# Later conditioning of a hybrid decoder trunk: sums over the partitions by VectorE's block transposes, and one matmul for up to three parts

## The chip, the core and the metric

One NeuronCore of one Trainium2 chip runs the whole program. The metric is the device time of one execution in microseconds (us). In this text PE is TensorE's matrix part and PEld its weight loads, DVE is VectorE, ACT is ScalarE, POOL is GpSimd and SP is SyncE, whose queue issues most DMAs. L12 is line 12 of the kernel before, unless the text says that it is of the changed one.

## The reference

Four layers of a decoder trunk on x of 1024 positions by 1024 features, in float32. Layer i uses one mixer: layers 0 and 3 HGRN2 (a gated linear recurrence), layer 1 attention with a sliding window (SWA), layer 2 gated DeltaNet (GDN). A conditioning vector c sets a shift, a scale and a gate for each layer:

```
mod = (c @ ada_w[i] + ada_b[i])[:, None, :]        # 1024 x 3072 weights for each layer
shift, scale, gate = jnp.split(mod, 3, axis=-1)
h = rmsnorm(x, norm_g[i]) * (1.0 + scale) + shift
x = x + gate * mixer(h)
```

The change touches the first of these lines alone, for most of the layers: the vector times matrix product that gives the 3072 numbers of `mod`.

## The kernel before

The activations lie with features on the 128 partitions. The 3072 columns of `ada_w[i]` are worked in six parts of 512: parts 0 and 1 are the shift, 2 and 3 the scale, 4 and 5 the gate. Parts 0 to 3 of layer 0 are needed at once and go through `ada_first`, which neither version changes. The other twenty parts (4 and 5 of layer 0, all six of layers 1, 2 and 3) are the later conditioning. It is the generator `ada` (L407), which runs as a side stream beside the mixer of the layer before: `weave` takes a step of it now and then, 18 or 8 steps for each head of HGRN2, 16 for each group of SWA, 10 for each head of GDN, and what is left is drained at the mixer's end. Parts 4 and 5 of layer 0 and all of layer 1 run in layer 0, those of layer 2 in layer 1, those of layer 3 in layer 2.

A part has nine steps. In eight of them a tile of 128 rows by 512 columns of the matrix is loaded (L415) and DVE adds the tile, times c of that row, to the sum `acc` (L403, L405). Now acc holds, for each partition, a sum over eight rows; what is still to do is the sum over the 128 partitions, with the result turned so that columns come to lie on partitions. In the ninth step `ada_cols` (L421) does both by matmuls: four pieces of acc, 128 by 128 each, are the weights, a column of ones is the moving operand, and four columns of results come out in PSUM (L426). DVE adds the bias and writes them to `mod` (L428). After parts 2 and 3 DVE also makes `gcol`, the norm's weight times one plus scale (L432). `acc` has one buffer. The order of the parts is 2, 0, 3, 1, 4, 5.

Three resources are shared with the mixers:

- The matrix tiles are loaded into the tag "raw" of the pool wp, three buffers of 128x512. All weights come through the same three: `load_w` (L160) loads a raw tile, ACT rounds it to the part `w_hi` (L171), DVE makes the rest `w_lo` (L172), and three matmuls (L196 to L198) use the two parts. Those have four buffers each.
- The results of L426 go to a PSUM bank of the tag "tr", of which there is one. HGRN2's transposes `kh_ps` (L1077) and `ot_ps` (L1109), SWA's `qt_ps` (L1296) and GDN's transposes use it too.
- `eye32` (made at L272) is a constant of 128x128 that both versions have: four copies side by side and on top of each other of the identity of 32 by 32.

The order of instructions on each engine is set by a scheduler that places them by priority and by its own costs; each engine then works through its queue in that order. HGRN2's state matmul `s_ps` (L1092), SWA's query gate `sw_zs` (L1280) and HGRN2's `hg_zs` (L971) are the neighbours of which the prediction speaks.

## Time and profile before

| what | value |
|---|---|
| median of 3 runs | 2759.97 us (2746.81 to 2761.26) |
| the profiled execution | 2755.2 us |
| its span, first to last instruction | 2753.5 us |
| PE, DVE, ACT busy | 97%, 73%, 45% |
| the later conditioning's matmuls, first and last start | 135.9 and 1831.7 us |

The profile is that of one execution. A row of a group of instructions names the line, engine, operation, the tiles written and read and how many there are, then the busy time and the mean duration, and then the engine's idle time in front of them with what ended it. A row of the timeline gives the start, the duration, the engine and what it did, with an idle time ahead of it in brackets. A row of the waits names who waited for whom: the total, how many times, the longest. A row of windows gives the stretch, its length, and the busy time of PE, PEld, DVE, ACT and POOL, then PE's granted clock, the DMA share and GB/s.

### The profile page before, as it was taken

Reading aid. Unit: us, or ns where it says so; the run is one execution under the profiler, and the core shown is the slowest. Engines: PE = TensorE matmul, PEld = TensorE weight load, DVE = VectorE, ACT = ScalarE, POOL = GpSimd, SP = SyncE. Lnnn points to the kernel's source line nnn. Section 1 sums busy time; section 2 is a strip of 40 time slices with the busy share of each in tenths; the row PEclk is TensorE's granted clock in tenths of the full one; section 3 lists DMA queues with packets and bytes.
Section 4 is the critical chain, followed back from the end, with each engine's and each line's share of the span. In section 5 each row is a group of like instructions: output and inputs, shape, how many; then the busy total and the mean of one; then the engine's idle time right before and its main releaser. Section 6 shows DMA issues by size and latency. Waiting matters only on the chain.

```text
span 2753.5 us, 51775 instructions
## 1 busy us (share of the span) xinstructions
PE 2662.9 (97%) x19217; PEld 2147.3 (78%) x19217; DVE 1997.0 (73%) x5669; ACT 1235.4 (45%) x3139; POOL 136.5 (5%) x352
## 2 busy tenths in 40 slices
PE   8999999999999999899999999999999999999999
PEld 4878888778878767677787887787778888887877
DVE  6675765778677777777898898988775757556575
ACT  4332333344445565444445555555543434333342
POOL 0000100000000000001001001100000001000000
PEclk9999999999999999999999999999999999999999
DMA  6232222344223243334343343432454211111133
GB/s 240 77 104 79 70 79 76 109 133 150 58 89 100 74 147 93 111 82 107 97 127 85 104 126 93 124 101 80 142 183 127 85 51 43 51 43 51 46 119 112
DMA packets 347667, 273.30 MB, mean 99 GB/s; under 512 B 68964, under 2 KB 276247, under 8 KB 347415
## 3 DMA queue, kind: packets, MB, share of 16 engines
q1 hardware_dynamic: 347126, 268.95, 32.7%
q8 instruction: 151, 2.47, 0.4%
q14 instruction: 102, 0.83, 0.1%
q0 software_dynamic: 288, 1.05, 0.1%
HBM read 224.77 MB, written 45.15 MB: 98 GB/s over the span
## 4 chain that ended last, share of the span: by engine, by line
PE 74%; DVE 12%; DMA 6%; ACT 4%; issue 2%; SPq 0%; POOL 0%; DVEq 0%; ACTq 0%; POOLq 0%
PE proj_ps L196 10%; PE proj_ps L197 10%; PE proj_ps L198 10%; PE outp_ps L196 4%; PE outp_ps L198 4%; PE outp_ps L197 4%; PE projt_ps L196 3%; PE projt_ps L198 3%; PE projt_ps L197 3%; DMA ada_w<-in_ada_w_dram 2%; PE pv_ps L1340 1%; DVE gd_tb L617 1%; DVE w_lo L172 1%; DMA o_in<-od 1%; PE w_ps L859 1%
## 5 line engine op out<-in xcount | busy, mean ns | idle before, releaser
L196 PE MATMUL proj_ps<-hhi,w_hi 128*128 128x512 f32 x1664 | 682.2, 410 | 11.6 <-ACT gd_tb L615 8.4
L198 PE MATMUL proj_ps<-hhi,w_lo 128*128 128x512 f32 x1664 | 677.6, 408 | 1.3 <-issue 1.3
L197 PE MATMUL proj_ps<-hlo,w_hi 128*128 128x512 f32 x1664 | 676.8, 407 | 0.0
L196 PEld LDWEIGHTS proj_ps<-hhi,w_hi 128*128 128x128 f32 x1664 | 316.1, 190 | 69.4 <-ACT gd_tb L615 11.2
L198 PEld LDWEIGHTS proj_ps<-hhi,w_lo 128*128 128x128 f32 x1664 | 315.7, 190 | 57.7 <-issue 1.9
L197 PEld LDWEIGHTS proj_ps<-hlo,w_hi 128*128 128x128 f32 x1664 | 315.8, 190 | 56.3 <-issue 1.6
L172 DVE TENSOR_TENSOR w_lo<-w_raw,w_hi 128x512 fp32r<-128x512 f32 x332 | 223.2, 675 | 165.6 <-ACT w_hi L171 136.7
L171 ACT CAST w_hi<-w_raw 128x512 fp32r<-128x512 f32 x332 | 201.7, 611 | 293.6 <-PE proj_ps L197 167.9
L197 PE MATMUL projt_ps<-w_lo,hhi 128*128 128x256 f32 x896 | 257.4, 290 | 4.1 <-DVE w_lo L172 4.1
L196 PE MATMUL projt_ps<-w_hi,hhi 128*128 128x256 f32 x896 | 257.6, 290 | 0.8 <-ACT w_hi L171 0.8
L198 PE MATMUL projt_ps<-w_hi,hlo 128*128 128x256 f32 x896 | 256.1, 289 | 0.0
L196 PE MATMUL outp_ps<-o_hi,w_hi 128*128 128x512 f32 x576 | 229.1, 400 | 4.7 <-ACT o_hi L1166 3.6
L198 PE MATMUL outp_ps<-o_hi,w_lo 128*128 128x512 f32 x576 | 228.0, 398 | 1.6 <-DVE w_lo L175 1.6
L197 PE MATMUL outp_ps<-o_lo,w_hi 128*128 128x512 f32 x576 | 229.2, 399 | 0.2
L197 PEld LDWEIGHTS projt_ps<-w_lo,hhi 128*128 128x128 f32 x896 | 171.1, 192 | 7.1 <-DVE w_lo L172 5.2
L196 PEld LDWEIGHTS projt_ps<-w_hi,hhi 128*128 128x128 f32 x896 | 171.0, 192 | 4.2 <-ACT w_hi L171 1.2
L198 PEld LDWEIGHTS projt_ps<-w_hi,hlo 128*128 128x128 f32 x896 | 171.0, 192 | 2.7 <-issue 1.4
L617 DVE SCALAR_TENSOR_TENSOR gd_tb<-gd_xs,taps,gd_tb 128x512 f32<-128x512 f32 x192 | 144.3, 752 | 25.2 <-ACT gd_tb L615 21.3
L174 ACT ACTIVATE w_hi<-w_raw,par 128x512 fp32r<-128x512 f32 (+1 forms) x136 | 94.7, 698 | 140.1 <-PE outp_ps L197 95.5
L196 PEld LDWEIGHTS outp_ps<-o_hi,w_hi 128*128 128x128 f32 x576 | 108.6, 189 | 29.0 <-ACT o_hi L1166 5.7
L198 PEld LDWEIGHTS outp_ps<-o_hi,w_lo 128*128 128x128 f32 x576 | 109.0, 190 | 24.7 <-DVE w_lo L175 2.2
L175 DVE SCALAR_TENSOR_TENSOR w_lo<-w_raw,par,w_hi 128x512 fp32r<-128x512 f32 (+1 forms) x136 | 96.8, 716 | 41.6 <-ACT w_hi L174 39.9
(389 smaller groups left out, 4923.3 us busy)
## 6 DMA issues: line engine op xcount, KB each, us to landing
ada_w<-in_ada_w_dram SPq DMA_DIRECT2D x160, 256.0 KB, 2.8
w_raw<-in_hg_in_w_dram SPq DMA_DIRECT2D x136, 256.0 KB, 2.9
w_raw<-in_gd_in_w_dram SPq DMA_DIRECT2D x108, 256.0 KB, 3.0
o_in<-od SPq DMA_DIRECT2D x72, 256.0 KB, 3.4
w_raw<-in_gd_out_w_dram SPq DMA_DIRECT2D x64, 256.0 KB, 2.8
w_raw<-in_sw_in_w_dram SPq DMA_DIRECT2D x48, 256.0 KB, 3.0
w_raw<-in_hg_out_w_dram SPq DMA_DIRECT2D x40, 256.0 KB, 2.9
ada_w<-in_ada_w_dram SPq DMA_DIRECT2D x8, 1024.0 KB, 9.5
```

Source lines behind the costliest of these rows:

```text
L171: nc.scalar.copy(hi, raw)
L172: nc.vector.tensor_tensor(lo, raw, hi.bitcast(F32), ALU.subtract)
L174: nc.scalar.activation(hi, raw, AF.Copy, scale=scale)
L175: nc.vector.scalar_tensor_tensor(lo, raw, scale, hi.bitcast(F32), ALU.mult, ALU.subtract)
L196: mm(out, a[0], b[0], start=start, stop=False)
L197: mm(out, a[0], b[1], start=False, stop=False)
L198: mm(out, a[1], b[0], start=False, stop=stop)
L617: nc.vector.scalar_tensor_tensor(y, xs[:, j:j + HT], w(j), y, ALU.mult, ALU.add)
L859: nc.tensor.matmul(po[:, hd[a]], dd["u"][a, hf][:, cs], rhs, start=True, stop=True)
L1340: nc.tensor.matmul(po[a * 64:(a + 1) * 64], vg[:, n + 1 - nkb + b, :], p4[:, :, a, :], start=b == 0, stop=b == nkb - 1)
```

## The change

The ninth step of a part is done by DVE. It transposes the sum in blocks of 32 by 32 (128x512 to 128x512, into a tile `ada_t` that is taken from the tag "raw"), and sums each run of 32 in a row: 128x16 numbers, written to a third of the tile `red`. After the last part of a group one matmul with `eye32` as the weights adds the four groups of 32 partitions for all parts of the group at once (32 or 48 columns). The result has each block of 32 columns on all four groups of partitions; four adds, each on 32 partitions, pick from it what belongs there and add the bias. Groups are parts 4 and 5 of layer 0, and parts 0 to 2 and 3 to 5 of the layers behind. The eight columns of `gcol` are made after parts 3 to 5, by one step. The numbers of steps are the same.

```diff
+        p0, p1 = parts[0], parts[-1] + 1
+        red = self.adap.tile([P, 3, 16], F32, name="ada_red", tag="red", bufs=1)[:, :p1 - p0]
         for part in parts:
...
-            self.ada_cols(i, part, acc)
+            at = self.wp.tile([P, HT], F32, name="ada_t", tag="raw", bufs=RAW)
+            nc.vector.transpose(at, acc)
+            nc.vector.tensor_reduce(red[:, part - p0, :], at.rearrange("p (j r) -> p j r", r=32), AX.X, ALU.add)
+            if part == parts[-1]:
+                pm = self.psum("tr", "ada_ps", 1)[:, :16 * (p1 - p0)]
+                nc.tensor.matmul(pm, self.eye32, red.rearrange("p a j -> p (a j)"), start=True, stop=True)
+                pv = pm.rearrange("p (a m) -> p a m", m=4)
+                for m in range(4):
+                    ms = slice(m * 32, (m + 1) * 32)
+                    nc.vector.tensor_tensor(self.mod[ms, i, 4 * p0:4 * p1], pv[ms, :, m], self.adab[ms, i * 24 + 4 * p0:i * 24 + 4 * p1], ALU.add)
+                if p1 == 6 and p0 < 4:
+                    self.scales(i, 0, 8)
             yield 1
...
-            side = k.ada(i, ADA_ORDER[4:])
+            side = k.ada(i, (4, 5))
         if nxt is not None:
-            side = chain(side, k.ada(nxt, ADA_ORDER))
+            side = chain(side, k.ada(nxt, (0, 1, 2)), k.ada(nxt, (3, 4, 5)))
```

`scales` makes `gcol` as L432 did; `ada_first` still ends in `ada_cols`.

What it does to the order is shown at two places. The first is PE's queue near the end of layer 0, where layer 1's last part before, and its last group of three parts now, is summed over the partitions. `kh_ps` is a transpose of HGRN2 into the bank "tr", `lev_ps` are products of its chunk. Before:

```order
L198 MATMUL proj_ps<-hhi,w_lo 128x512
L426 MATMUL ada_ps<-ones,ada_acc 128x1 x4
L1077 MATMUL kh_ps<-ident,hg_kg 128x128 x4
L1092 MATMUL s_ps<-hg_v,hg_kht 128x128
L1060 MATMUL lev_ps<-hg_X,hg_kg 32x96
```

And in the changed kernel:

```order
L1076 MATMUL lev_ps<-hg_X,hg_kg 32x32
L426 MATMUL ada_ps<-ada_red,eye_569 128x48
L1093 MATMUL kh_ps<-ident,hg_kg 128x128 x4
L1108 MATMUL s_ps<-hg_v,hg_kht 128x128
L195 MATMUL outp_ps<-o_hi,w_hi 128x512
```

One matmul of 48 columns stands where four of one column stood, and the transpose into the same bank is still the next instruction. The four matmuls of each of the five parts ahead are gone from their places, but for one such matmul for parts 0 to 2.

The second place is DVE's queue at the end of layer 1, where the last part of layer 2's conditioning is done. `sw_st`, `sw_sm` and `rs_t`, `rs_y` belong to SWA's softmax and norms. Before:

```order
L172 TENSOR_TENSOR w_lo<-w_raw,w_hi 128x512
L1324 TENSOR_TENSOR sw_st<-sw_st 128x4
L151 TENSOR_SCALAR rs_y<-q_ms 128x16
L1325 TENSOR_SCALAR sw_st<-sw_st 128x4
L153 SCALAR_TENSOR_TENSOR rs_t<-rs_y,q_ms 128x16
L428 TENSOR_TENSOR mod<-ada_ps,adab 128x4
L1326 RECIPROCAL sw_st<-sw_st 128x4
```

And in the changed kernel (its line 404 is the accumulation, 422 and 423 are the transpose and the sum, 430 the adds, 448 the scales):

```order
L404 SCALAR_TENSOR_TENSOR ada_acc<-ada_w,par,ada_acc 128x512 x2
L422 STREAM_TRANSPOSE ada_t<-ada_acc 128x512
L423 TENSOR_REDUCE ada_red<-ada_t 128x16
L1296 SCALAR_TENSOR_TENSOR sw_zs<-sw_tmp,proj_ps 128x512
L171 TENSOR_TENSOR w_lo<-w_raw,w_hi 128x512
L171 TENSOR_TENSOR w_lo<-w_raw,w_hi 128x256
L171 TENSOR_TENSOR w_lo<-w_raw,w_hi 128x512
L430 TENSOR_TENSOR mod<-ada_ps,adab 32x12 x4
L171 TENSOR_TENSOR w_lo<-w_raw,w_hi 128x256
L1296 SCALAR_TENSOR_TENSOR sw_zs<-sw_tmp,proj_ps 128x512
L448 SCALAR_TENSOR_TENSOR gcol<-mod,par 128x8
```

Where the sum's result was one add among SWA's small steps, the transpose and the sum now stand directly behind the last accumulation step, then four blocks of other work (a gate and three weight splits), then the four adds.

More of the change, by code (lines that the diff above doesn't have):

```diff
@@ L43 @@
 NS = 8, 16, 10
-ADA_ORDER = (2, 0, 3, 1, 4, 5)
 AO = ((2, True), (0, True), 0, D, (3, True), (1, True))
@@ L429, in ada_cols, with scales @@
         if part in (2, 3):
-            g0 = c0 - 8
-            g = self.par[:, i * 8 + g0:i * 8 + g0 + 4]
-            nc.vector.scalar_tensor_tensor(self.gcol[:, i, g0:g0 + 4], self.mod[:, i, c0:c0 + 4], 1.0, g, ALU.add, ALU.mult)
+            self.scales(i, c0 - 8, 4)
+    def scales(self, i, g0, n):
+        g = self.par[:, i * 8 + g0:i * 8 + g0 + n]
+        self.nc.vector.scalar_tensor_tensor(self.gcol[:, i, g0:g0 + n], self.mod[:, i, 8 + g0:8 + g0 + n], 1.0, g, ALU.add, ALU.mult)
     def shift(self, i, k):
```

## The prediction

> **What bounds the kernel now.** I read the page first: the busy shares, then the chain of work that ended last, from which these two lines come.

> ```profile
> PE 2662.9 (97%) x19217; PEld 2147.3 (78%) x19217; DVE 1997.0 (73%) x5669; ACT 1235.4 (45%) x3139; POOL 136.5 (5%) x352
> PE 74%; DVE 12%; DMA 6%; ACT 4%; issue 2%; SPq 0%; POOL 0%; DVEq 0%; ACTq 0%; POOLq 0%
> ```

> TensorE (PE) is busy for 97% of the span and makes 74% of the chain. The later conditioning runs beside the mixers of layers 0, 1 and 2, from about 95 to 1832 us, so I asked for the busy times of that stretch, and for what PE waits for in it (total us, times, longest).

> ```profile
> 95.00:1832.00 1737.00, 1674.62 (x11906) 1353.56 (x11907) 1318.70 (x3771) 811.79 (x2173) 87.35 (x206) 0.99 0.35 101
> PE proj_ps L196 <- ACT gd_tb L615: 8.4, 4, 5.8
> PE projt_ps L197 <- DVE w_lo L172: 4.1, 4, 1.4
> PE ot_ps L1109 <- DVE hg_tmp L1105: 3.9, 6, 1.3
> ```

> In 1737 us PE is busy for 1674.6, so it is idle for 62.4 us; the three longest waits are small and spread. VectorE (DVE) is busy for 1318.7 us and idle for 418. Whatever stands in PE's queue there is paid nearly in full; what is added to DVE has room on average, and hurts only where PE waits for DVE.

> **What the change removes from PE.** Each of the twenty later parts ends in four matmuls of one column whose weights are a 128x128 piece of the sum. The trace writes two records for each float32 matmul, so 160 of the 192 below are these (the other 32 belong to the four parts before layer 0, which stay). First the rows of that tile, then one such part in PE's timeline.

> ```profile
> L426 PEld LDWEIGHTS ada_ps<-ones,ada_acc x192: 181/192/192, 25.9 to 1831.7; 128*128 128x128 f32 x160, 1*128 1x128 f32 x32
> L426 PE MATMUL ada_ps<-ones,ada_acc x192: 164/250/271, 25.9 to 1831.7; 128*128 128x1 f32 x160, 1*128 1x1 f32 x32
> L428 DVE TENSOR_TENSOR mod<-ada_ps,adab x24: 152/161/164, 27.0 to 1832.0; 128x4 f32<-128x4 f32 x24
> ```

> ```profile
> 135.48 0.39 PE L197 MATMUL proj_ps<-hlo,w_hi 128*128 128x512 f32 x1
> 135.71 0.39 PE L198 MATMUL proj_ps<-hhi,w_lo 128*128 128x512 f32 x1
> 135.94 0.95 PE L426 MATMUL ada_ps<-ones,ada_acc 128*128 128x1 f32 x8
> 136.75 0.49 PE L196 MATMUL proj_ps<-hhi,w_hi 128*128 128x512 f32 x1
> 137.07 0.39 PE L197 MATMUL proj_ps<-hlo,w_hi 128*128 128x512 f32 x1
> ```

> Projection matmuls start 0.23 us apart. From the one at 135.71 to the second one behind it (137.07) are 1.36 us, where 0.46 would do: a part costs PE 0.90 us. Twenty make 18.0 us.

> **What it adds to PE.** Seven float32 matmuls with 128x128 weights and 48 or 32 columns: one for parts 4 and 5 of layer 0, six for the half layers of three parts. The nearest row is HGRN2's state matmul of 128 columns between projections.

> ```profile
> 239.91 0.40 PE L196 MATMUL proj_ps<-hhi,w_hi 128*128 128x512 f32 x1
> 240.14 0.38 PE L1092 MATMUL s_ps<-hg_v,hg_kht 128*128 128x128 f32 x2
> 240.28 0.48 PE L197 MATMUL proj_ps<-hlo,w_hi 128*128 128x512 f32 x1
> 240.60 0.40 PE L198 MATMUL proj_ps<-hhi,w_lo 128*128 128x512 f32 x1
> 240.83 0.40 PE L196 MATMUL proj_ps<-hhi,w_hi 128*128 128x512 f32 x1
> ```

> Three projection steps take 0.92 us there instead of 0.69: 0.23 for one such matmul, 1.6 us for seven. PE's queue is shorter by 16.4 us. The order bears out that this happens: seven matmuls stand where eighty stood.

> **The bank they share.** The result goes to the one PSUM bank of the tag "tr", where the mixers' transposes go too. Two of the twenty parts have such a transpose right behind them; here are both.

> ```profile
> 529.15 0.95 PE L426 MATMUL ada_ps<-ones,ada_acc 128*128 128x1 f32 x8
> 530.35 0.66 PE L1077 MATMUL kh_ps<-ident,hg_kg 128*128 128x128 f32 x4 [0.25 <-DVE mod L428]
> ...
> 990.76 0.92 PE L426 MATMUL ada_ps<-ones,ada_acc 128*128 128x1 f32 x7
> 991.93 0.63 PE L1296 MATMUL qt_ps<-ident,sw_q 128*64 128x128 f32 x4 [0.26 <-DVE mod L428]
> ```

> The transpose starts 1.20 and 1.17 us behind the first ada matmul instead of 0.81, as it waits for DVE's add: about 0.4 each, 0.8 together. In the new order two of the seven have one right behind too (the same kh_ps and qt_ps), and now four adds of 32 partitions must read the bank, with one or more blocks of other DVE work ahead of them in the queue. From nothing more than today to 1.8 us more each (two blocks of 0.6 and four adds of 0.16, estimates from the rows below and above): 0 to 3.6 us more. I take 0.8, since DVE does those blocks while it would otherwise sit idle in front of the bank. The new matmul also waits for the last sum, with all of PE's queue behind it. At the end of layer 1 the sum stands only just ahead: 0 to 1.2 us there, of which I take nothing, since the old matmuls waited for their sums nowhere in this stretch either.

> **What it adds to DVE.** Twenty 32x32 block transposes of 128x512, twenty sums of 128x512 to 128x16, and 28 small adds for 20; three scale steps for six. Both large kinds occur elsewhere, and the timeline shows how 512-wide operations follow each other.

> ```profile
> L763 DVE STREAM_TRANSPOSE gd_Uc<-gd_Tc 128x512 f32<-128x512 f32 x8 | 5.6, 701 | 1.9 <-ACT gd_Tc L761 1.9
> L1233 DVE TENSOR_REDUCE q_ms<-sw_tmp 128x8 f32<-128x512 f32 x16 | 10.9, 681 | 18.5 <-ACT sw_tmp L1232 18.5
> ```

> ```profile
> 249.11 0.69 DVE L1105 TENSOR_TENSOR hg_tmp<-o_ps,rs_y 128x512 f32<-128x512 f32 x1
> 249.72 0.68 DVE L971 TENSOR_TENSOR hg_zs<-proj_ps,hg_tmp 128x512 f32<-128x512 f32 x1
> 250.31 0.68 DVE L172 TENSOR_TENSOR w_lo<-w_raw,w_hi 128x512 fp32r<-128x512 f32 x1
> 250.91 0.68 DVE L1112 TENSOR_TENSOR hg_tmp<-ot_ps,hg_zs 128x512 f32<-128x512 f32 x1
> ```

> Such operations last 0.68 to 0.70 us and start 0.60 apart. A part adds 1.2 us, twenty add 24.0; eight more small adds and three scale steps less, at the 0.16 of the add's row, add 0.8: 24.8 us. [...]

> Against that stands an idle time that mostly goes. In the stretch DVE waits in front of the old add for PE's four matmuls, with its whole queue behind it (row: total us, times, longest).

> ```profile
> DVE mod L428 <- PE ada_ps L426: 18.6, 15, 3.5
> ```

> That is 0.93 us for a part; seven groups keep 6.5, so 12.1 go. DVE's net is 24.8 less 12.1, 12.7 us in 1737. Bounds on what PE sees: all of it, 12.7, or nothing; in the mean 62.4 us of PE idle stand against 1318.7 us of DVE work, 4.7%, and that gives 0.6. I take 1, because transpose and sum stand close together and so delay by 1.2 us what waits behind them.

> **What it does to the loads.** The transposed block lies in one of the three raw buffers through which all weights come (tag "raw"). A load behind it goes out one release later, and the third behind it waits for the sum. That ring is always full.

> ```profile
> SPq L169 <- DVE w_lo L172: 616.4, 161, 27.3
> DVE ada_acc L405 <- DMA ada_w<-in_ada_w_dram: 22.4, 24, 2.6
> ACT w_hi L171 <- PE proj_ps L197: 167.9, 110, 4.2
> ```

> ```profile
> ada_w<-in_ada_w_dram SPq DMA_DIRECT2D x160, 256.0 KB, 2.8
> ```

> SyncE's queue waits for DVE to free a buffer 161 times; a load needs 2.8 us to land. Cover there is: the casts wait 110 times for PE to give back the split weights, so raw weights mostly lie ready. But 24 accumulation steps already wait for their load, 0.93 us each, and DVE's queue waits with them. If each of the twenty blocks adds one such wait, that is 18.7 us of DVE idle: all of it, or nothing, on PE; at the same 4.7%, 0.9. I take 1. The conditioning's parts come in another order (0, 1, 2 and 3, 4, 5), and the scales of a layer now come with its last group; in the new order this is still some ninety DVE rows ahead of the norm that reads them, so it costs nothing.

> **The sum.** 18.0 less 1.6 gives 16.4 off PE; 0.8 for the bank, 1 for DVE and 1 for the ring come back: 13.6 us. The profiled execution took 2755.2 us (span 2753.5): 2741.6, said as 2742. The median of the three runs, 2759.97, lies 4.8 above it, but the lowest, 2746.81, lies 8.4 below, and the mean of all four is 2755.8, so I do not move it. About 0.5% (13.8 us) is what a measurement of this kernel can tell from no change.

> **Rival 1: half the gain is lost, the time is the same.** Only 74% of the chain is PE. If PE's queue is what decides in that share alone, 12.1 of the 16.4 count; with 12% of DVE's 12.7 (1.5), 6% of the ring's 18.7 (1.1) and the bank's 0.8 the gain is 8.7 us: 2746.5. For it speaks the row of 24 waits for loads; against it that PE idles only 62.4 us in 1737 and that the matmuls around the removed ones start 0.23 us apart with no gap. [...]

> **Rival 2: slower, by the raw ring.** The block sits in a buffer until its sum is done, the next loads come late, DVE stands in front of an accumulation step, and splits and mixer steps behind it reach PE late. With the full price on PE a part costs 1.2 (transpose and sum) and 0.93 (a load's wait): 42.6 us for twenty, less 16.4: 26 slower, 2781. It decides from 0.82 us a part on. Against it: the casts' 110 waits for PE, and that the old add's 0.93 of DVE idle cost PE nothing visible but the two bank waits.

> **Another order around it.** The scheduler places hundreds of other rows differently now. Single PE waits of the stretch reach 5.8 us; two such waits more or fewer, an estimate of 8 us either way, go into the range. That the change does not do what it says is excluded by the order.

> **How the numbers follow.** Forecast 0.55, rival 1 0.34, rival 2 0.11. Low end: 16.4 with every cost hidden and 8 us of better order, 2730.8, said as 2730. High end: DVE's 12.7 in full and half the ring's 18.7 on top of a gain of 16.4 gives 2761, and 4 for the spread of the runs: 2765. It holds the forecast and rival 1 and leaves out rival 2. Faster by over 0.5%: 0.53, as the forecast lies near that bound of the profiled time and past it of the median; same 0.36; slower 0.11.

> **What would show it.** Right: the matmuls of ada_ps fall to 46 records; transposes of 0.70 and sums of 0.68 us, twenty each; DVE's wait in front of the adds falls from 18.6 to about 7 us; PE idle in the stretch stays near 62 us while the stretch shrinks by 13. Rival 1: PE idle grows by 5 or more. Rival 2: DVE's waits for ada_w and PE's for w_lo double. The forecast is wrong if PE's idle in the stretch grows by more than 8 us, or if the time lies above 2756.

## The result and the profile after

The change makes the kernel faster: 2728.97 us in the median of six runs (2726.77 to 2734.83) against 2759.39 for the kernel before in six runs on the same chip. The ratio, which is that of the means, is 0.9902 with a 95% interval of 0.9883 to 0.9921, so 22 to 32 us less, about 27. The forecast was 2742, about 14 less than the profiled execution of the kernel before. The profiled execution took 2734.63 us, 20.6 less than the 2755.2 before.

The page of the changed kernel gives the span, the busy shares and the engines of the chain, and the view of cores gives the granted clock.

```profile
span 2732.9 us, 51521 instructions
...
PE 2647.5 (97%) x19071; PEld 2133.6 (78%) x19071; DVE 2019.3 (74%) x5714; ACT 1235.5 (45%) x3139; POOL 132.6 (5%) x352
...
PE 73%; DVE 15%; DMA 6%; ACT 3%; issue 2%; SPq 0%; DVEq 0%; ACTq 0%
```

```profile
core 0: 2732.9 us, clock 0.991
```

PE has 146 matmul records fewer, 160 less the 14 of the seven new matmuls, and 15.4 us less busy time. DVE has 22.3 us more. PE is still busy for 97% of the span. The granted clock of the kernel before was higher in its profiled execution:

```profile
core 0: 2753.5 us, clock 0.993
```

The stretch beside the three mixers, from the same start to the last group's matmul, in the view of windows:

```profile
95.00:1812.00 1717.00, 1658.51 (x11779) 1340.06 (x11779) 1342.63 (x3820) 813.99 (x2176) 84.60 (x206) 0.99 0.35 102
```

It is 20.0 us shorter. PE is busy for 16.1 us less and idle for 58.5 instead of 62.4; DVE is busy for 23.9 us more. So the stretch shrank by more than PE's queue did, and PE's idle time, which was to stay, fell by 3.9.

The new instructions, by their tiles (duration in ns, shortest, median, longest):

```profile
L430 DVE TENSOR_TENSOR mod<-ada_ps,adab x28: 148/165/177, 167.5 to 1812.5; 32x12 f32<-32x12 f32 x24, 32x8 f32<-32x8 f32 x4
...
L426 PE MATMUL ada_ps<-ada_red,eye x14: 190/273/310, 167.1 to 1809.5; 128*128 128x48 f32 x12, 128*128 128x32 f32 x2
```

```profile
L422 DVE STREAM_TRANSPOSE ada_t<-ada_acc x20: 692/705/712, 123.2 to 1792.5; 128x512 f32<-128x512 f32 x20
L423 DVE TENSOR_REDUCE ada_red<-ada_t x20: 665/682/687, 123.9 to 1793.2; 128x16 f32<-128x512 f32 x20
```

PE's timeline around the first of the new matmuls:

```profile
166.92 0.39 PE L197 MATMUL proj_ps<-hhi,w_lo 128*128 128x512 f32 x1
167.15 0.30 PE L426 MATMUL ada_ps<-ada_red,eye 128*128 128x32 f32 x2
167.28 0.48 PE L195 MATMUL proj_ps<-hhi,w_hi 128*128 128x512 f32 x1
167.60 0.40 PE L196 MATMUL proj_ps<-hlo,w_hi 128*128 128x512 f32 x1
```

From the projection at 166.92 to the second one behind it are 0.68 us, where 0.46 would do: 0.22 us for one new matmul, as the state matmul had let one expect.

The waits around the conditioning (total us, times, longest), first those of PE, then those of DVE:

```profile
PE projt_ps L196 <- DVE w_lo L171: 4.7, 5, 1.4
...
PE kh_ps L1093 <- DVE mod L430: 1.5, 1, 1.5
...
PE qt_ps L1312 <- DVE mod L430: 1.2, 2, 0.9
```

```profile
DVE ada_acc L404 <- DMA ada_w<-in_ada_w_dram: 31.4, 31, 2.3
...
DVE mod L430 <- PE ada_ps L426: 4.0, 2, 2.8
```

DVE's wait in front of the adds fell from 18.6 to 4.0 us. Its wait for the matrix tiles grew from 22.4 to 31.4. PE's wait for the split weights hardly moved (4.1 before). The bank costs more than before. The timeline of PE at both places, then that of DVE at both, show why:

```profile
522.02 0.42 PE L426 MATMUL ada_ps<-ada_red,eye 128*128 128x48 f32 x2
523.94 0.63 PE L1093 MATMUL kh_ps<-ident,hg_kg 128*128 128x128 f32 x4 [1.49 <-DVE mod L430]
...
977.84 0.31 PE L426 MATMUL ada_ps<-ada_red,eye 128*128 128x48 f32 x2
979.04 0.60 PE L1312 MATMUL qt_ps<-ident,sw_q 128*64 128x128 f32 x4 [0.89 <-DVE mod L430]
```

```profile
521.94 0.63 DVE L174 SCALAR_TENSOR_TENSOR w_lo<-w_raw,par,w_hi 128x384 fp32r<-128x384 f32 x1
522.49 0.68 DVE L987 TENSOR_TENSOR hg_zs<-proj_ps,hg_tmp 128x512 f32<-128x512 f32 x1
523.09 0.70 DVE L430 TENSOR_TENSOR mod<-ada_ps,adab 32x12 f32<-32x12 f32 x4
...
978.19 0.71 DVE L430 TENSOR_TENSOR mod<-ada_ps,adab 32x12 f32<-32x12 f32 x4 [1.21 <-PE ada_ps L426]
```

At the first place a split and a gate step stand ahead of the four adds in DVE's queue, and PE stands in front of the bank until the adds are done. At the second DVE has done its blocks and is idle for 1.21 us until the new matmul has ended; there PE waits for the four adds alone, 0.71 us in a row where the old add took 0.16. The next matmul can start 0.13 us behind the new one (167.15 to 167.28 above); here the transposes start 1.92 and 1.20 us behind it, so 1.8 and 1.1 us are lost, where about 0.4 each was lost before.

### The profile page after: what moved, and what is told of

The parts are those of the page before. It is cut to its first block, busy times and chain, and to the rows that moved or that the text cites. A ratio compares the mean times of both kernels' runs of the same rounds, so it can differ in the third digit from the quotient of the medians.

```text
span 2732.9 us, 51521 instructions
## 1 busy us (share of the span) xinstructions
PE 2647.5 (97%) x19071; PEld 2133.6 (78%) x19071; DVE 2019.3 (74%) x5714; ACT 1235.5 (45%) x3139; POOL 132.6 (5%) x352
## 4 chain that ended last, share of the span: by engine, by line
PE 73%; DVE 15%; DMA 6%; ACT 3%; issue 2%; SPq 0%; DVEq 0%; ACTq 0%
PE proj_ps L196 10%; PE proj_ps L195 10%; PE proj_ps L197 10%; PE outp_ps L195 4%; PE outp_ps L197 4%; PE outp_ps L196 4%; DMA ada_w<-in_ada_w_dram 3%; PE projt_ps L195 3%; PE projt_ps L197 3%; PE projt_ps L196 3%; DVE w_lo L171 1%; PE pv_ps L1356 1%; DVE gd_tb L633 1%; PE ada_row L391 1%; PE w_ps L875 1%
## 5 line engine op out<-in xcount | busy, mean ns | idle before, releaser
L197 PE MATMUL proj_ps<-hhi,w_lo 128*128 128x512 f32 x1664 | 680.5, 409 | 0.0
L196 PE MATMUL proj_ps<-hlo,w_hi 128*128 128x512 f32 x1664 | 675.2, 406 | 0.0
L196 PEld LDWEIGHTS proj_ps<-hlo,w_hi 128*128 128x128 f32 x1664 | 315.8, 190 | 58.6 <-issue 2.4
L197 PEld LDWEIGHTS proj_ps<-hhi,w_lo 128*128 128x128 f32 x1664 | 315.9, 190 | 56.4 <-issue 1.0
L171 DVE TENSOR_TENSOR w_lo<-w_raw,w_hi 128x512 fp32r<-128x512 f32 x332 | 223.4, 675 | 158.2 <-ACT w_hi L170 132.5
L196 PE MATMUL projt_ps<-w_lo,hhi 128*128 128x256 f32 x896 | 258.7, 291 | 4.7 <-DVE w_lo L171 4.7
L197 PE MATMUL projt_ps<-w_hi,hlo 128*128 128x256 f32 x896 | 256.8, 290 | 0.0
L196 PE MATMUL outp_ps<-o_lo,w_hi 128*128 128x512 f32 x576 | 229.2, 399 | 0.0
L197 PE MATMUL outp_ps<-o_hi,w_lo 128*128 128x512 f32 x576 | 227.9, 398 | 0.8 <-DVE w_lo L174 0.8
L196 PEld LDWEIGHTS projt_ps<-w_lo,hhi 128*128 128x128 f32 x896 | 171.1, 192 | 8.1 <-DVE w_lo L171 6.0
L197 PEld LDWEIGHTS projt_ps<-w_hi,hlo 128*128 128x128 f32 x896 | 170.8, 192 | 2.3 <-issue 1.0
L404 DVE SCALAR_TENSOR_TENSOR ada_acc<-ada_w,par,ada_acc 128x512 f32<-128x512 f32 x140 | 104.5, 746 | 32.4 <-DMA ada_w<-in_ada_w_dram 31.4
## 6 DMA issues: line engine op xcount, KB each, us to landing
ada_w<-in_ada_w_dram SPq DMA_DIRECT2D x160, 256.0 KB, 2.7
w_raw<-in_hg_in_w_dram SPq DMA_DIRECT2D x136, 256.0 KB, 2.8
w_raw<-in_gd_in_w_dram SPq DMA_DIRECT2D x108, 256.0 KB, 3.1
o_in<-od SPq DMA_DIRECT2D x72, 256.0 KB, 3.2
w_raw<-in_gd_out_w_dram SPq DMA_DIRECT2D x64, 256.0 KB, 2.8
w_raw<-in_sw_in_w_dram SPq DMA_DIRECT2D x48, 256.0 KB, 2.9
w_raw<-in_hg_out_w_dram SPq DMA_DIRECT2D x40, 256.0 KB, 2.8
```

Of the source, the lines that this page charges most:

```text
L171: nc.vector.tensor_tensor(lo, raw, hi.bitcast(F32), ALU.subtract)
L196: mm(out, a[0], b[1], start=False, stop=False)
L197: mm(out, a[1], b[0], start=False, stop=stop)
L404: self.nc.vector.scalar_tensor_tensor(acc, w, c, acc, ALU.mult, ALU.add)
```

## The experiments

Twelve kernels were run, in four sets. Each ratio is to the kernel before on the same chip. The expectations weigh these theories. **A** is the prediction's: PE's queue is paid in full, 0.90 us for a part's four matmuls, and what is added to DVE costs next to nothing. **B** says that DVE's wait in front of the old add cost PE more than the four matmuls show. **C** says that the scheduler's other placing of everything else makes the difference between the forecast and the result. A+, in the expectations of e5 and e8, adds up what e4 and e3 had measured, 21 us and 6 us less. Rival 2 is that of the prediction, the raw ring.

| kernel | median us | ratio to before | 95% interval | us from before at full clock |
|---|---|---|---|---|
| e1, order of the parts alone | 2760.09 | 0.9997 | 0.9976 to 1.0019 | −2.2 ± 1.6 |
| e2, matmuls twice | 2792.14 | 1.0119 | 1.0088 to 1.0150 | +15.7 ± 3.1 |
| e3, transpose and sum added to before | 2752.02 | 0.9977 | 0.9958 to 0.9996 | −7.6 ± 1.8 |
| e4, before without the matmuls | 2737.75 | 0.9923 | 0.9896 to 0.9950 | −22.8 ± 1.9 |
| e5, the change again | 2731.76 | 0.9911 | 0.9893 to 0.9929 | −24.7 ± 2.6 |
| e6, ring buffer held in before | 2756.12 | 0.9999 | 0.9984 to 1.0014 | −4.2 ± 1.7 |
| e7, two DVE passes added to before | 2762.56 | 1.0017 | 1.0002 to 1.0033 | −3.2 ± 1.3 |
| e8, the change, transpose and sum twice | 2737.98 | 0.9929 | 0.9910 to 0.9948 | −23.3 ± 2.9 |
| e9, the change, another bank | 2728.73 | 0.9912 | 0.9890 to 0.9934 | −26.6 ± 1.5 |
| e10, the change, a matmul for each part | 2742.13 | 0.9961 | 0.9947 to 0.9975 | −15.3 ± 2.3 |
| e11, before, placed anew | 2759.06 | 1.0023 | 1.0007 to 1.0039 | +3.1 ± 1.5 |
| e12, the change, placed anew | 2736.07 | 0.9952 | 0.9934 to 0.9970 | −15.3 ± 1.8 |

The last column is worked out from the span and the granted clock that each run lists: the two multiplied, the mean over a kernel's runs, less the same for the kernel before on that chip, with twice the standard error. It leaves out the time that runs lose by a lower clock. For the kernel before on the chip of e1 to e4 it narrows the standard deviation of a run from 6.6 to 3.1 us.

### What the four matmuls cost: e2 and e4

In e2 the kernel before issues the four matmuls of each later part twice.

```diff
-        for j in range(4):
+        for j in list(range(4)) * times:   # times = 2 for the later parts
```

> The kernel before with the four matmuls of each of the twenty parts issued twice, the second four over the first. A: 0.81 us more a part on PE, 16 us slower, and with it 16 us more of DVE idle in front of the adds, of which 1 reaches PE: +17. B: the DVE idle reaches PE by a good part: +22 to +32. C: not foretold, off +17 by 6 or more either way.

Measured: 1.0119, about 33 us more. Its page and its view of cores:

```profile
PE 2701.6 (97%) x19377; PEld 2182.7 (78%) x19377; DVE 1994.7 (71%) x5669; ACT 1235.6 (44%) x3139; POOL 135.5 (5%) x352
```

```profile
core 0: 2789.8 us, clock 0.985
```

The granted clock is 0.985 here against 0.993. A span times what is missing to full clock gives the time lost to it: 41.8 us here, 19.3 before. Without that, PE is busy for 16 us more, which is A's term for another 80 matmuls. Over all six runs it is 15.7 us, in the table's last column. By the time alone 33 us lies above A's 17 and just above B's range; half of it is lost clock, which no theory had. The six runs had 0.983 to 0.988 and the 23 of the kernel before 0.986 to 0.996, so the lower clock goes with this kernel, but that it comes from the extra matmuls was not shown.

In e4 the kernel before goes without the four matmuls of the twenty later parts; the add reads four columns of the sum instead, so the sum over partitions is left out.

```diff
-        pm = self.psum("tr", "ada_ps", 1)
-        for j in range(4):
+        pm = self.psum("tr", "ada_ps", 1) if mm else acc   # mm False for the later parts
+        for j in range(4 * mm):
```

> The kernel before without the matmuls of the twenty later parts; the sum over the partitions is left out, and the add reads four columns of the partial sum instead, so DVE no longer waits for PE there. A: 18.0 off PE, 0.8 for the two bank waits and 0.9 for DVE's idle: -19.7. B: DVE's 18.6 us of idle count for more: -26 to -38. C: off -19.7 by 6 or more either way.

Measured: 0.9923, about 21 us less. Its page:

```profile
PE 2648.3 (97%) x19057; PEld 2134.9 (78%) x19057; DVE 1997.9 (73%) x5669; ACT 1236.8 (45%) x3139; POOL 131.5 (5%) x352
```

DVE's waits for the old matmuls are gone with them, but for the four parts ahead of layer 0:

```profile
DVE mod L428 <- PE ada_ps L426: 10.6, 4, 4.3
```

The gain is that of PE's queue, with no more for DVE's 18.6 us of idle that also went. That speaks for A and against B. The change takes the same from PE, less its seven matmuls, and gained at least as much.

### What is added to DVE and to the ring: e3, e6, e7, e8

In e3 the kernel before makes the transpose and the sum as well, in the raw ring, and nothing reads their result.

```diff
             self.ada_cols(i, part, acc)
+            red = self.adap.tile([P, 16], F32, name="ada_red", tag="red", bufs=1)
+            at = self.wp.tile([P, HT], F32, name="ada_t", tag="raw", bufs=RAW)
+            nc.vector.transpose(at, acc)
+            nc.vector.tensor_reduce(red, at.rearrange("p (j r) -> p j r", r=32), AX.X, ALU.add)
```

> The kernel before, with the transpose and the sum added to each of the twenty parts behind the old matmuls, the transposed block in the raw ring as in the changed kernel; their result is not used. A: 24 us of DVE work and twenty turns of the ring, of which 2 to 3 us reach PE: +2.5. The rival of the prediction (all of it on PE): +43. B: as A. C: off +2.5 by 6 or more.

Measured: 0.9977, 6 us less, with 24 us more work for DVE. At full clock it is 7.6 us less. That is off A's +2.5 by more than 6, as C had it: what makes an addition faster is most likely the order of the rest. e6 and e7 took its two halves apart. In e6 the part takes a raw buffer and copies 16 columns into it; in e7 DVE makes two passes over the sum in place, with no buffer.

```diff
+            at = self.wp.tile([P, HT], F32, name="ada_t", tag="raw", bufs=RAW)   # e6
+            nc.vector.tensor_copy(at[:, 0:16], acc[:, 0:16])
...
+            for _ in range(2):                                                  # e7
+                nc.vector.tensor_tensor(acc, acc, acc, ALU.max)
```

> The kernel before; each of the twenty parts also takes one raw buffer behind its old matmuls and writes 16 columns of it by a short DVE copy, without transpose or sum. If the 6 us that adding transposes and sums gave come from the ring (a load held back by one turn collides less with the mixer): -5 to -8. If they come from where the scheduler puts the rest (theory C): any value within 8 us, and not that of the run before by rule. If the ring costs, as the prediction says: +1 to +3.

> The kernel before with two passes of DVE over the partial sum, in place, ahead of the old matmuls of each of the twenty parts: some 25 us of DVE work, no buffer of the ring, the same result. A: 4.7% of it reaches PE, +1 to +3. Prediction's rival 2: +25. Theory C: anything within 8 us, as with the transposes (-6).

Measured: 0.9999 for the ring alone and 1.0017, 5 us more, for DVE's work alone. The 5 us are lost clock: the twelve runs of e7 have a mean granted clock of 0.989 and the kernel before 0.992, and at full clock e7 takes 3 us less. Whether DVE's work made the clock lower was not shown. In e8 the change makes transpose and sum twice.

```diff
-            nc.vector.transpose(at, acc)
-            nc.vector.tensor_reduce(red[:, part - p0, :], ...)
+            for _ in range(2):
+                nc.vector.transpose(at, acc)
+                nc.vector.tensor_reduce(red[:, part - p0, :], ...)
```

> The changed kernel with each transpose and sum done twice: 24 us more of DVE work, the ring's buffer held 1.2 us longer. A and A+: 1 to 3 slower than the changed kernel, so -24 to -26 from before if that stands at -27. Rival 2: 24 slower than the changed kernel. Theory C: up to 8 either way.

Measured: 0.9929, against 0.9911 for the change itself on the same chip: 5 us more, and the two intervals overlap. At full clock it is 1.4 us, less than the errors. A further 40 operations were worth 24 us to rival 2. The ring and DVE's work, together or apart, moved the time by −6 to +5 us, and at full clock none of the four kernels shows a cost: rival 2 falls.

### The change once more, and its parts: e5, e9, e10

e5 is the changed kernel unaltered, so that e6 to e8 stand beside it.

> The changed kernel, to stand on one chip with the runs beside it. Taking the matmuls away gave -21 and adding transposes and sums gave -6. Theory A+ (these two add up): -27. Theory A as predicted: -14 to -18.

Measured: 0.9911, 23 us less in the medians and 24 in the means, nearer to A+ than to A as predicted. In e9 the result goes to the tag "lev", which has two banks, so that no transpose waits for the adds.

```diff
-                pm = self.psum("tr", "ada_ps", 1)[:, :16 * (p1 - p0)]
+                pm = self.psum("lev", "ada_ps", 2)[:, :16 * (p1 - p0)]
```

> The changed kernel with the seven matmuls' results in the tag lev, which has two banks, in place of tr, which has one. If the two waits of transposes for the bank (1.5 and 0.9 us of PE idle in the changed kernel's profile) are a cost of their own: 2 us faster than the changed kernel, -26 to -29 from before. Theory C: up to 8 either way from the changed kernel.

Measured: 0.9912, no gain over the change, where 2 us were expected. Of its PE waits for the adds one is left, and it is longer than both of the change's together:

```profile
PE s_ps L1327 <- DVE mod L430: 3.5, 1, 3.5
```

The bank wait moved to SWA's scores, which use the other tag. In e10 each part has a matmul of its own, twenty in all, as if it were a group.

```diff
-            side = k.ada(i, (4, 5))
+            side = chain(k.ada(i, (4,)), k.ada(i, (5,)))
-            side = chain(side, k.ada(nxt, (0, 1, 2)), k.ada(nxt, (3, 4, 5)))
+            side = chain(side, *(k.ada(nxt, (a,)) for a in range(6)))
```

> The changed kernel without groups: each of the twenty parts has its own matmul (16 columns) and its own four adds. A: thirteen matmuls more at 0.23, 3.0 us on PE, 52 small adds and thirteen more waits of DVE for PE, of which 1 reaches PE: 4 slower than the changed kernel, -21 to -23 from before. Theory B: 8 or more slower.

Measured: 0.9961, 13 us above e9 on the same chip (11 at full clock). A had said 4, and the number is one that B named, 8 or more. Thirteen more matmuls of 0.22 us would be 2.9 us. The busy row of its page shows more than that on PE:

```profile
PE 2656.1 (97%) x19097; PEld 2139.2 (78%) x19097; DVE 2028.5 (74%) x5766; ACT 1235.8 (45%) x3139; POOL 137.2 (5%) x352
```

At a granted clock of 0.991, as in the change's profile, PE is busy for 8.6 us more. B's way is not seen, though: DVE waits for these matmuls for 5.2 us where the change has 4.0, and the span less PE's busy time is 83.9 us where the change has 85.4. Where the other 6 us on PE lie, and the rest of the 13, was not found: grouping the parts is worth keeping, but the durations of the matmuls do not say why.

### The placing of everything else: e1, e11, e12

In e1 the kernel before works its parts in the order of the change.

```diff
-ADA_ORDER = (2, 0, 3, 1, 4, 5)
+ADA_ORDER = (0, 1, 2, 3, 4, 5)
```

> The kernel before with the parts in the order 0, 1, 2, 3, 4, 5; everything else is as before. Theory A (PE's queue is shorter by 16.4 us, and some 3 us of DVE, ring and bank come back): the same within 3 us. Theory B (the four matmuls cost more than their 0.90 us on PE, since all of DVE's queue stands behind the add that waits for them): the same within 3 us. Theory C (the measured gain beyond the sum comes from how the scheduler places the other rows once something near them has moved): a change of 6 us or more, either way.

Measured: 0.9997, no difference (2 us less at full clock). e11 and e12 are the kernel before and the changed one with other numbers of side steps beside the mixers. No work is added or taken away, but the scheduler lays both kernels out anew.

```diff
-NS = 8, 16, 10
+NS = 9, 18, 9
```

> The kernel before with 9, 18 and 9 steps of the conditioning for each head or group of the three mixers in place of 8, 16 and 10: the same instructions, placed elsewhere. A: the same within 2 us. Theory C (placing alone moves the time by some us): off by 3 to 8, and PE's idle time in the profile below the 81.7 us (between matmuls) of the kernel before, as in every other re-placed kernel so far (76 to 79).

> The changed kernel with 9, 18 and 9 steps of the conditioning in place of 8, 16 and 10, as the kernel before had them in the run before this one (which was 6 slower than the kernel before). If the gain beyond the predicted 14 is luck of one placing: 13 to 19 faster than that run, so -7 to -13 from before. If the change is worth 24 to 27 wherever the rest is placed: -18 to -21 from before.

Measured: 1.0023 for before, 6 us more (3 at full clock), and 0.9952 for the change, 13 us less. The 6 us are in C's range, but PE's idle time did not fall as C expected. The 13 us lie at the edge of the first expectation of e12, so part of the gain beyond 14 is that of one placing. The change is worth the ratio of the two: 0.993, about 20 us in this placing (0.990 to 0.995, an estimate from the two intervals), where it was worth 24 and 27 in its own. At full clock it is 18 in this placing and 25 in its own (e5). Page and view of cores of before placed anew:

```profile
PE 2666.3 (97%) x19217; PEld 2149.2 (78%) x19217; DVE 1996.8 (72%) x5669; ACT 1239.1 (45%) x3139; POOL 135.1 (5%) x352
```

```profile
core 0: 2756.8 us, clock 0.991
```

And of the change placed anew:

```profile
PE 2649.6 (97%) x19071; PEld 2134.3 (78%) x19071; DVE 2018.1 (74%) x5714; ACT 1235.9 (45%) x3139; POOL 132.8 (5%) x352
```

```profile
core 0: 2734.7 us, clock 0.991
```

At one clock, PE is busy for 16.7 us less, and the span less PE's busy time falls from 90.5 to 85.1: 5.4 less. e11 also speaks against B. Its DVE waits for the old matmuls far longer than that of the kernel before (29.7 us over the whole span, 20 times):

```profile
DVE mod L428 <- PE ada_ps L426: 52.4, 21, 8.8
```

PE's idle time did not follow: the span less its busy time is 90.5 us against 90.6.

A group of six parts, or a buffer of its own for the transposed block, wasn't tried.

## Why the prediction was right, and where it was wrong

PE's time can be split in the same way for each kernel: busy by the page, the part of it lost to the clock (summed from the trace's clock records), and the span less busy.

| kernel | span | PE busy | lost to the clock | busy less lost | span less busy |
|---|---|---|---|---|---|
| before | 2753.5 | 2662.9 | 19.6 | 2643.3 | 90.6 |
| the change | 2732.9 | 2647.5 | 25.3 | 2622.2 | 85.4 |
| e4, no matmuls | 2734.7 | 2648.3 | 23.2 | 2625.1 | 86.4 |
| e2, matmuls twice | 2789.8 | 2701.6 | 41.9 | 2659.7 | 88.2 |
| e11, before anew | 2756.8 | 2666.3 | 24.3 | 2642.0 | 90.5 |
| e12, the change anew | 2734.7 | 2649.6 | 24.5 | 2625.1 | 85.1 |

**What bounds the kernel: right.** PE's queue is paid in full. e4 takes 18.2 us of PE work at full clock, e2 adds 16.4, where twenty times 0.90 is 18.0.

**The new matmuls: right.** 0.22 us measured, 0.23 expected. PE's term was 16.4 net; the pair placed anew shows 16.9 at full clock, the change's own pair 21.1. The 4.7 above the term in the change's own pair are not in the pair placed anew, so they are not the matmuls'.

**What is given back: the step that failed.** The sum let 2.8 us come back to PE (0.8 for the bank, 1 for DVE, 1 for the ring), and its check was that PE idle in the stretch "stays near 62 us". It fell to 58.5, and over the whole span by 5.2 us in one placing and 5.4 in the other. Point by point:

- The bank was mis-sized: 1.8 and 1.1 us are lost in front of it, where 0.8 was lost before: 2.1 us more, in place of the 0.8 that the sum took. At kh_ps DVE did not do the blocks ahead of the adds while it would otherwise have stood idle; they stood in PE's way. At qt_ps it did, as the prediction had it, and the four adds themselves were the cost. e9 shows that another bank moves this wait and does not remove it.
- DVE's own work was right, 23.9 us for 24.8, and its wait fell by 14.6 instead of 12.1. Nothing of it is seen on PE: e3 and e8 put the same work on DVE once more and found −6 and +5 us, and −8 and +1 at full clock. The timeline at the last part has the transpose, the sum and the next step 0.73 and 0.61 us apart:

```profile
1792.48 0.70 DVE L422 STREAM_TRANSPOSE ada_t<-ada_acc 128x512 f32<-128x512 f32 x1
1793.21 0.69 DVE L423 TENSOR_REDUCE ada_red<-ada_t 128x16 f32<-128x512 f32 x1
1793.82 0.34 DVE L877 TENSOR_SCALAR gd_wg<-w_ps,gd_gm 128x128 f32<-128x128 f32 x1
```

  That is 1.34 us for the part, where 1.2 was expected; the next step starts 0.08 us before the sum has ended.
- The ring's cost to PE was right, its way was not. The wait for matrix tiles grew by 9 us, half of the bound of 18.7, but not by the ring. The same row in e3, which takes the same twenty buffers, and in e4, which takes none and only lacks the matmuls:

```profile
DVE ada_acc L405 <- DMA ada_w<-in_ada_w_dram: 22.9, 27, 2.3
...
DVE ada_acc L405 <- DMA ada_w<-in_ada_w_dram: 28.2, 29, 2.3
```

  e3 has about the 22.4 of the kernel before; most of the growth comes with the loss of the matmuls. The 110 waits of the casts that the prediction set against it are those of the whole span; the stretch has 56.
- What the sum did not have is that four of PE's waits elsewhere would go. In the kernel before they are

```profile
PE o_ps L1088 <- POOL hg_at L1054: 2.1, 1, 2.1
PE proj_ps L196 <- DVE sw_zs L1280: 2.0, 1, 2.0
PE w_ps L859 <- ACT gd_v L685: 1.9, 2, 1.7
...
PE outp_ps L198 <- DVE w_lo L175: 1.6, 1, 1.6
```

  7.6 us together. In the change only the last is left, with 0.8. Through the other kernels these four rows come to 3.5 to 8.7 us in every one that has the four matmuls (before, e1, e2, e3, e6, e7, e11) and to 0.7 to 1.8 in every one that has not (the change, e4, e5, e8 to e10, e12). Yet the span less PE's busy time of e1, e3, e6 and e7 is 85.2 to 87.3 us, hardly more than the change's 85.4, so other waits went there. That the four go with the matmuls is a count over the kernels, made after the rows were seen to go. At three of the four no add stands in DVE's queue in the 7 us ahead, so it is not simply DVE's wait for PE; why they go was not found.

**"Another order around it": right as a bound, wrong as a term.** 8 us either way went into the range and 0 into the sum. (Two waits of the 5.8 us that it names would be 11.6; the 8 is not worked out from them.) Edits of the kernel before that take no work away moved it by −6 to +6 us by their ratios (e1, e3, e6, e7, e11), and by −8 to +3 at full clock. The change's own placing is a good one: 24 and 27 us there, 20 in the other. So of the 27 us some 16 to 18 are PE's queue. About 5 are PE's idle time, which fell in both placings; but it fell nearly as far in e1, e3, e6 and e7, which keep the matmuls, so this part is not shown to be the change's own. The last few are not in the other placing, and how they divide between order and clock stays open. C holds at most for what goes beyond PE's queue, not for the whole gain.

**Rival 1: wrong.** The gain was not halved: the removed PE time counted whole. The weight loads were busy for 78% of the span before and after. e4 took weight loads away together with the matmuls, so no run here parts the two.

**Rival 2: wrong**, by e3, e6 and e8.

**The range.** Its low end, 2730, was set from the profiled execution with 8 us of better order. The measured 2728.97 lies a microsecond below it: the forecast was right in its sign and in its main term, PE's queue, and took half of the gain. The other half is in no term of the sum; the range reached so near to it only by the 8 us for another order.

## What to carry to other kernels

Where the tensor engine is busy to 97%, count what small matmuls cost between their neighbours, not by their size: four of one column took 0.90 us of its queue, twenty sets of them 18 us, and the same sums on an engine with idle time (here DVE, busy to 73%) moved the time by −6 to +5 us, with no cost to be seen at full clock. Where a scheduler lays the whole program out anew after an edit, expect some 0.2% in either direction from that alone, and compare both kernels in a second placing before a difference of that size is read as the edit's. Compare runs and profiles at the same granted clock, or take the lost time out first: here that removed nearly all of the 5 us that DVE's work seemed to cost, and half of what doubled matmuls did.

## What the runs showed of the hardware

One thing was not expected: why the same kernel spreads. The runs of the kernel before on one chip went from 2750.06 us at a granted clock of 0.996 to 2776.93 at 0.986. In the traces of the kernel before and of the changed one the clock records hold only full and half speed. But for the last record of each, half speed comes in 8 and 9 stretches of 3.41 us, twice that or three times that. In one stretch of the kernel before the projection matmuls start 0.43 us apart (1582.71 to 1583.99 us), where they start 0.23 apart at full speed. Where half speed begins can be read in the windows around the bank wait at kh_ps in the changed kernel (PE's busy time is the first number behind the length, the clock the third from the end):

```profile
518.30:521.70 3.40, 3.40 (x35) 2.55 (x35) 3.28 (x13) 1.13 (x3) 1.35 (x3) 1.00 0.30 98
521.70:525.10 3.40, 1.37 (x17) 0.89 (x13) 2.65 (x10) 2.05 (x6) 0.71 (x3) 1.00 0.54 182
525.10:528.50 3.40, 3.26 (x9) 2.58 (x10) 1.83 (x4) 1.74 (x4) 0.00 (x0) 0.50 0.47 128
528.50:531.90 3.40, 3.40 (x18) 2.73 (x18) 1.75 (x4) 1.24 (x2) 0.00 (x0) 1.00 0.59 191
```
